# The last down product of a three-block transformer kernel as seven block products, with weight sums made in DRAM

## The chip, the cores and the metric

The kernel runs on one core of one Trainium2 chip. The metric is the device time of one execution in microseconds (us). The kernel before takes 3527.75 us, the median of three runs (3526.47 to 3527.91).

## The reference

Three pre-norm blocks follow one another on a sequence of 1024 tokens with 1024 features, all in float32. Cut to what matters here:

```python
def first_block(x, ...):       # 16 meta tokens ahead of x
    p = rms_norm(h) @ w_in     # q, k, v, g, gate rank, conv channels
    mix = concat(gla_branch(q, k, v, g, gr), short_conv_branch(cb, cc, cx))
    h = h + mix @ w_out;  h = h + relu(rms_norm(h) @ w_up) ** 2 @ w_down
def second_block(x, ...):      # three mixers, then a gated FFN with a convolution
def third_block(x, c, ...):
    x = x + gate1 * rms_norm_3(mix, norm1_post)
    h = rms_norm_3(x, norm2_pre) * (1.0 + scale2) + shift2
    f = jnp.square(jax.nn.relu(h @ w_fc1)) @ w_fc2
    return x + gate2 * rms_norm_3(f, norm2_post)
```

The FFNs are called f1, f2 and f3 in the kernel. The change concerns `f @ w_fc2` of the third block: a hidden vector of 4096 features times a 4096 x 1024 matrix, for 1024 tokens.

## The kernel before, in words

Features lie on partitions, so a tensor of 1024 x 1024 is eight tiles [128, 1024], or in halves of 512 tokens. A float32 product is made of three matmuls of rounded halves: with w = whi + wlo and x = Hh + Hl, `mm3` (L428) issues Hh·whi, Hl·whi and Hh·wlo into one accumulation in PSUM. Each weight unit of 512 KB is loaded by SP into a tile `raw` (L183) and split by `split` (L336): ACT copies it to `whi`, and DVE subtracts to get `wlo`. The class `Stream` holds the list of all units of the program in order. `tick` splits the next one when its load is some microseconds of PE time old, and `_split` (L203) then loads on, two units ahead.

**The FFNs.** `up7` (L895) makes an up product in groups. Of four blocks (two of output features by two of tokens) it needs seven block products instead of eight, with sums of weight blocks made by DVE on the raw tiles. For f1 and f3 every finished block goes through ReLU and square on ACT and from there to a DRAM tile `gd` (its issue is L910, from ACT). There are 16 groups; the first 12 of f3 take one piece from an earlier pass through the DRAM tile `sd` (L963). `down7` (L1029) makes the down product in chunks of 2, 2 and then 4 hidden tiles: the H tiles come back from `gd` as units of their own and are split into Hh and Hl, every chunk multiplies them with its weights for all eight output tiles, and `add` adds the sums to X, the first time by an ACT copy, later by DVE (L305). That is 32 hidden tiles x 8 output tiles x 2 halves x 3 = 1536 matmuls of 128x512. In f1 and f2 the residual is added by accumulating DMAs from POOL (L1066). In f3 it is loaded by SP into spare slots and a tile `hp` (both named `xr`), and `tail` normalises each half and writes the output, the second half in two parts of 256 tokens.

**The first block** is where the scheduler puts new rows. SP loads x (`xin`, eight loads of 256 or 512 KB) and the first weights; ACT squares x (`xs`), DVE makes the row factors (`rs`, `rr`, `xt`), ACT rounds the normed x (`Hh`). Then come the projections for v, q and k, g (`mm` into `V`, `kk`, `q`, `sg`) and the conv channels (`c1`: `cct`, `yt`). `gla` (L1348) is a generator that runs beside the projections, in four groups of 256 tokens, gi = 0 to 3. Each group has seven levels: `elem` (L1378) makes a factor `f` (POOL subtracts, ACT takes the exponential, DVE multiplies twice), `pairs` (L1428) makes eight small matmuls into each of two PSUM tiles `pa` and copies them into `At` by two DVE `copy_predicated` (L1437). States `hs` are carried by DVE; at a group's end `po` collects the output on PE and `norm` scales it into `sg`. After the first block's projections o1 multiplies `yt` and `sg` by w_out (into `X0`, `X1`).

**What sets the order.** The program is written in one order of calls, with generators advanced beside the matmuls by an estimate of PE time (`pe`). The framework's scheduler then orders the instructions of each engine by priorities and its own estimate of times, and gives every buffer and DMA a semaphore. Engines run their instructions in that order, and an instruction that waits holds those behind it.

## Time and profile before

| what | value |
|---|---|
| median of three runs | 3527.75 us |
| the profiled execution | 3526.44 us, of which span 3524.6 us |
| PE busy | 3419.4 us, 97% of the span, 16725 matmuls |
| DVE, ACT, POOL busy | 62%, 39%, 10% |
| mean granted clock of TensorE | 0.983 of full speed |
| DMA | 421.46 MB, mean 120 GB/s |

The busy time of PE is of modelled ends, but with 97% the matmuls follow one another nearly everywhere: a matmul less is worth its step, and a wait costs only where PE stands. The stages that the text speaks of lie at 0 to 60 us (start), 60 to 400 us (projections and GLA of the first block), 2843 to 3135 us (f3 up), 3135 to 3510 us (f3 down) and 3510 us to the end (tail).

### The profile page before, as it was taken

What the parts mean: (1) busy time and instruction counts of PE and PEld (TensorE: products, weight loads), DVE (VectorE), ACT (ScalarE), POOL (GpSimd) and SP (SyncE); (2) the same over time, 40 slices, a digit from 0 to 9 for tenths busy, and PEclk for the clock granted to TensorE, in tenths of its full rate; (3) what the DMA queues carried; (4) which work ended last, traced back from release to release, by engine and by line L of the source; (5) the groups of instructions that cost most, each with busy time, mean ns of one, the idle gap of its engine ahead of it and who ended that gap; (6) DMA issues with size and microseconds to landing.
All of it is one profiled execution on the core that took longest, in us unless ns stands there. A gap on an engine that the chain in (4) does not pass through costs nothing. (4 is left out here: it accounts for less than half of the span.)

```text
span 3524.6 us, 43683 instructions
## 1 busy us (share of the span) xinstructions
PE 3419.4 (97%) x16725; PEld 2808.1 (80%) x16725; DVE 2201.8 (62%) x3747; ACT 1367.4 (39%) x2046; POOL 335.8 (10%) x368
## 2 busy tenths in 40 slices
PE   7999999999999989999999999999999999999998
PEld 7788898887888777876698788878778878877887
DVE  5456366556666574667768988867665676645444
ACT  3432244444112443555634444431332564451111
POOL 0111020000000210000020000000232410000003
PEclk9999999999999999998999999999999999999999
DMA  3111444336633186444325322274222154343222
GB/s 106 48 43 47 148 135 148 117 118 191 184 133 113 58 196 173 123 129 147 110 94 166 116 84 84 96 221 149 88 67 90 62 184 149 132 167 114 96 84 72
DMA packets 180964, 421.46 MB, mean 120 GB/s; under 512 B 18088, under 2 KB 58744, under 8 KB 180628
## 3 DMA queue, kind: packets, MB, share of 16 engines
q1 hardware_dynamic: 133044, 325.34, 28.8%
q10 hardware_dynamic: 38304, 67.13, 5.1%
q0 software_dynamic: 9408, 26.22, 3.6%
q8 instruction: 131, 2.15, 0.3%
q14 instruction: 77, 0.63, 0.1%
HBM read 304.50 MB, written 105.63 MB: 116 GB/s over the span
## 5 line engine op out<-in xcount | busy, mean ns | idle before, releaser
L324 PE MATMUL mm<-Hh,whi 128*128 128x512 f32 (+3 forms) x3632 | 1384.2, 381 | 11.7 <-DVE X L305 4.5
L324 PE MATMUL mm<-Hh,wlo 128*128 128x512 f32 (+3 forms) x3632 | 1365.6, 377 | 4.7 <-DVE wlo L305 4.7
L324 PE MATMUL mm<-Hl,whi 128*128 128x512 f32 (+3 forms) x3632 | 1369.6, 377 | 0.2 <-DVE Hl L305 0.2
L324 PEld LDWEIGHTS mm<-Hh,whi 128*128 128x128 f32 x3632 | 686.0, 189 | 155.3 <-issue 6.8
L324 PEld LDWEIGHTS mm<-Hh,wlo 128*128 128x128 f32 x3632 | 685.7, 189 | 138.5 <-DVE wlo L305 9.0
L324 PEld LDWEIGHTS mm<-Hl,whi 128*128 128x128 f32 x3632 | 686.1, 189 | 127.7 <-issue 1.4
L319 ACT ACTIVATE whi<-raw 128x1024 fp32r<-128x1024 f32 (+3 forms) x386 | 379.0, 992 | 694.6 <-PE mm L324 459.9
L305 DVE TENSOR_TENSOR wlo<-raw,whi 128x1024 fp32r<-128x1024 f32 (+3 forms) x386 | 441.7, 1151 | 193.3 <-ACT whi L319 182.8
L305 DVE TENSOR_TENSOR X<-X,mm 128x512 f32<-128x512 f32 (+1 forms) x446 | 290.3, 655 | 366.7 <-PE mm L324 362.1
L324 PE MATMUL mm<-t,whi 128*128 128x512 f32 x1296 | 408.6, 396 | 2.4 <-ACT whi L319 2.4
L324 PEld LDWEIGHTS mm<-t,whi 128*128 128x128 f32 x1296 | 242.9, 188 | 62.4 <-ACT whi L319 3.3
L324 PE MATMUL mm<-t,wlo 128*128 128x512 f32 x648 | 256.7, 396 | 1.9 <-DVE wlo L305 1.7
L319 ACT ACTIVATE Hh<-raw 128x1024 fp32r<-128x1024 f32 x86 | 89.6, 1057 | 364.8 <-PE mm L324 213.3
L321 ACT ACTIVATE X<-X 128x512 f32<-128x512 f32 (+1 forms) x226 | 151.9, 673 | 186.2 <-DVE X L310 153.7
L305 POOL TENSOR_TENSOR acc<-acc,sq 128x256 f32<-128x256 f32 (+1 forms) x108 | 115.9, 1074 | 910.0 <-ACT sq L321 906.4
L305 DVE TENSOR_TENSOR raw<-raw 128x512 f32<-128x512 f32 x216 | 145.2, 687 | 79.5 <-DMA raw<-in_w_up 77.1
L324 PEld LDWEIGHTS mm<-t,wlo 128*128 128x128 f32 x648 | 121.8, 188 | 33.4 <-DVE wlo L305 4.1
L305 DVE TENSOR_TENSOR Hl<-raw,Hh 128x1024 fp32r<-128x1024 f32 x86 | 104.6, 1222 | 56.9 <-ACT Hh L319 56.3
L310 DVE SCALAR_TENSOR_TENSOR ada<-raw,silc,ada 128x128 f32<-128x128 f32 x336 | 115.5, 350 | 8.3
L324 PE MATMUL mm<-whi,Hh 128*128 128x264 f32 (+4 forms) x336 | 111.7, 342 | 6.5 <-ACT Hh L319 2.8
L324 PE MATMUL mm<-wlo,Hh 128*128 128x264 f32 (+4 forms) x336 | 111.2, 340 | 2.4 <-DVE wlo L305 2.4
L310 DVE SCALAR_TENSOR_TENSOR X<-mm,X 128x512 f32<-128x512 f32 x108 | 74.5, 690 | 61.6 <-PE mm L324 60.1
(290 smaller groups left out, 3400.0 us busy)
## 6 DMA issues: line engine op xcount, KB each, us to landing
raw<-in_w_up SPq DMA_DIRECT2D x136, 512.0 KB
raw<-gdf SPq DMA_DIRECT2D x86, 512.0 KB
raw<-in_w_down SPq DMA_DIRECT2D x86, 512.0 KB
gdf<-X ACTq DMA_DIRECT2D x108, 256.0 KB
raw<-in_w_ada SPq DMA_DIRECT2D x48, 512.0 KB
gdf<-X ACTq DMA_DIRECT2D x22, 512.0 KB
B<-qd SPq DMA_DIRECT2D x36, 256.0 KB
A<-qd SPq DMA_DIRECT2D x36, 256.0 KB
```

The source lines that it names most:

```text
L305: eng.tensor_tensor(out=out, in0=a, in1=b, op=op)
L310: self.nc.vector.scalar_tensor_tensor(out=out, in0=a, scalar=s, in1=b, op0=op0, op1=op1)
L319: self.nc.scalar.activation(out, in_, f, scale=scale, **kw)
L321: self.nc.scalar.activation(out, in_, f, bias=bias, scale=scale, **kw)
L324: self.nc.tensor.matmul(out, l, r, start=s, stop=e, skip_group_check=grp)
```

## The change

The down product of f3 is cut into blocks: two of hidden features by two of output features by two of tokens would be eight block products, and seven products P1 to P7 of sums of blocks give the same. Each has 8 pairs of units (`e`) x 4 output tiles x 2 x 3 = 192 matmuls, 1344 together.

- **Weights.** `_quarters` lays w_fc2 out by quarters. P1, P2 and P4 take a quarter as it is. P5, P6, P7 and P3 need sums of quarters, `sw[0]` to `sw[3]`, which `sums` (line 666 of the changed kernel) makes in DRAM: 16 copies of 1 MB issued from ACT, then 16 accumulating DMAs of 1 MB issued from POOL, of which eight add another quarter and eight add one finished sum to the next. In the source they stand ahead of the up product of f2, one at a time, 12 or 20 us of PE time apart.
- **Activations.** In the f3 up product each of the 16 groups makes four more DVE operations on 128x512 (two `tt`, two `stt`), 64 in all, and writes seven pieces of 256 KB to DRAM instead of four: three from ACT, four from POOL. Of the first 12 groups one piece is read back by POOL.
- **The down product.** `down_parts` walks P1, P2, P6, P7, P4, P5, P3. Each pair is a weight unit and a hidden unit of 512 KB, both split: 112 units, where `down7` had 64. PSUM sums run on over two products, and `out` makes X by an ACT copy or one DVE operation, so the adding up of chunks (L305, X<-X,mm) goes. Stream loads four units ahead.
- **The residual** is loaded by two POOL DMAs of 2 MB at the start of the down product, and the tail of the second half is one part of 512 tokens.

The core of the diff:

```diff
+    def sums(self, name, w):
+        S = self.S[name + "s"]
+        act, pool = self.nc.scalar, self.nc.gpsimd
+        for i, q in ((0, 1), (2, 1), (1, 0), (3, 2)):
+            for e in range(4):
+                self.sums_todo.append((act, 12.0, S[i, 2 * e:2 * e + 2], w[e, q], {}))
+        for i, q in ((0, 3), (2, 0), (1, None), (3, None)):
+            for e in range(4):
+                r = slice(2 * e, 2 * e + 2)
+                src = w[e, q] if q is not None else S[0 if i == 1 else 1, r]
+                self.sums_todo.append((pool, 20.0, S[i, r], src,
+                                       dict(accum_op=ALU.add, max_dma_last_dim=4096)))
+    def sums_step(self):
+        if self.sums_todo and self.pe >= self.sums_at:
+            eng, pace, dst, src, kw = self.sums_todo.pop(0)
+            eng.dma_start(out=dst, in_=src, **kw)
+            self.sums_at = self.pe + pace
...
-                relu2(v, v, 2 * g, 1)
+                if parts:
+                    relu2(v, v)
+                    t1_, t2_, t4_ = slot(), slot(), slot()
+                    self.tt(t1_, ca, v, ALU.subtract)
+                    self.tt(v, c22, v, ALU.subtract)
+                    self.stt(t2_, t1_, -1.0, c22, ALU.mult, ALU.subtract)
+                    self.stt(t4_, t2_, -1.0, c21, ALU.mult, ALU.subtract)
+                    for i, t in ((3, t1_), (5, v), (4, t2_), (6, t4_)):
+                        nc.gpsimd.dma_start(out=piece(i, g), in_=t)
...
+    def down_parts(self, name, out, tail):
+        W.ahead = 4
+        for n, i in enumerate(self.ORDER):
+            if n == 6:
+                self.drop_raws()
+                W.ahead = 2
+            if new:
+                ps = [self.ps() for _ in range(4)]
+            for e in range(8):
+                wa, wb = (W.get(u) for u in D_[8 * n + e])
+                for m in range(4):
+                    for k in (0, 1):
+                        w, x = slice(k * 512 + m * P, k * 512 + m * P + P), slice(k * 512, k * 512 + 512)
+                        self.mm3(ps[m], wa.hi[:, w], wa.lo[:, w], wb.hi[:, x], wb.lo[:, x],
+                                 new and e == 0 and k == 0, e == 7 and k == 1, not new)
...
+        self.sums("f3", a["w3_down"])
         self.up7("f2")
...
-        self.hp, e = self.pool("hp2", 1, None, "right")
+        xr = self.Hh.bitcast(F32)
+        for k in (0, 4):
+            nc.gpsimd.dma_start(out=xr[:, k:k + 4, :T], in_=self.xd[:, k:k + 4])
...
-        self.down7("f3", add, tail, quarters=True)
+        self.down_parts("f3", out, tail)
```

**Where the built program has the sums.** They depend on nothing but inputs, and the scheduler has put them at the start. On ACT, at the very start, before (whi is a rounded weight of v, Hh the rounded x, silc belongs to the third block):

```order
L321 ACT_TABLE_LOAD
L321 ACTIVATE xs_145<-xin_129 128x4x128
L321 ACTIVATE xs_146<-xin_129 128x4x128
L321 ACT_TABLE_LOAD
L321 ACTIVATE silc_62<-smalls_58 128x8
L319 ACTIVATE whi_151<-raw_137 128x1056
L321 ACT_TABLE_LOAD
L321 ACTIVATE rs_162<-rv_160 128x1
L321 ACTIVATE xs_171<-xin_129 128x4x128
L319 ACTIVATE whi_207<-raw_139 128x1056
L321 ACTIVATE xs_172<-xin_129 128x4x128
L319 ACTIVATE Hh_86<-xt_193 128x4x128
```

and now, from `rs` on (two xs, whi, two xs and whi stand ahead of it, and the first copy ahead of those):

```order
L334 ACT_TABLE_LOAD
L334 ACTIVATE rs_163<-rv_161 128x1
L334 ACT_TABLE_LOAD
L334 ACTIVATE silc_62<-smalls_58 128x8
L683 DMA swf3_103<-in_w3_down 16x16384
L334 ACT_TABLE_LOAD
L334 ACTIVATE rs_183<-rv_181 128x1
L332 ACTIVATE Hh_86<-xt_194 128x4x128
L332 ACTIVATE Hh_86<-xt_201 128x4x128
L332 ACTIVATE whi_230<-raw_156 128x1056
L332 ACTIVATE whi_236<-raw_212 128x1056
L683 DMA swf3_103<-in_w3_down 16x16384
```

The first Hh now stands behind two more table loads and the second of the 16 copies, whose DMA shares its semaphore with one of the x loads and waits for that. The other copies follow among the rows of the projections; the sixteenth stands right behind the exponential of f_1435 in group gi = 0.

On POOL, 14 of the 16 accumulates stand ahead of the GLA's first row; the last two stand among the rows of gi = 0. Before, from the fifth level of gi = 0 on (f_1659 is the first level of gi = 1):

```order
L305 TENSOR_TENSOR f_1505<-b_118 128x64x4 x2
L305 TENSOR_TENSOR ke_1794<-b_118 128x512
L305 TENSOR_TENSOR f_1565<-b_118 128x128x2 x2
L305 TENSOR_TENSOR f_1615<-b_118 128x256 x2
L305 TENSOR_TENSOR f_1659<-b_118 128x8x32 x2
```

and now:

```order
L683 DMA swf3_103<-swf3_103 256x1024
L318 TENSOR_TENSOR f_1506<-b_119 128x64x4 x2
L318 TENSOR_TENSOR f_1566<-b_119 128x128x2 x2
L318 TENSOR_TENSOR f_1616<-b_119 128x256 x2
L683 DMA swf3_103<-swf3_103 256x1024
L318 TENSOR_TENSOR f_1660<-b_119 128x8x32 x2
```

The last accumulate, which needs the last copy and an earlier accumulate to have landed, stands ahead of the first row of gi = 1.

On ACT the exponentials of gi = 1 have moved with it. Before they stood among the projections for sg and c1 (`cct`):

```order
L321 ACTIVATE f_1659<-f_1659 128x512
L321 ACT_TABLE_LOAD
L321 ACTIVATE sg_888<-mm_1590 128x512
L321 ACT_TABLE_LOAD
L321 ACTIVATE f_1714<-f_1714 128x512
L319 ACTIVATE whi_1678<-raw_1457 128x1024
L321 ACT_TABLE_LOAD
L321 ACTIVATE sg_888<-mm_1634 128x512
L321 ACT_TABLE_LOAD
L321 ACTIVATE f_1896<-f_1896 128x512
L319 ACTIVATE cct_1687<-mm_1689 128x348
```

and now (yt_3129 is the last tile of c1, whi_3463 a weight of o1):

```order
L332 ACTIVATE yt_3129<-cct_3128,smalls_58 128x1024
L332 ACTIVATE Hh_86<-yt_3129 128x512
L332 ACTIVATE whi_3463<-raw_3276 128x1024
L332 ACTIVATE Hh_86<-yt_3129 128x512
L334 ACT_TABLE_LOAD
L334 ACTIVATE f_1660<-f_1660 128x512
L334 ACTIVATE f_1715<-f_1715 128x512
L334 ACTIVATE ke_1795<-ke_1795 128x512
L334 ACTIVATE f_1897<-f_1897 128x512
L332 ACTIVATE kT_1883<-ax_1880 128x256
```

Groups gi = 1 to 3 stand behind the whole of c1, on every engine. DVE has their 42 `copy_predicated`, 36 products for `f`, 48 for `hs` and the rest in one run, and PE has from the last `mm` of c1 to the last `po` of gi = 3 their matmuls and 37 matmuls of o1, 24 of them ahead of the first `pa`.

## Rows read from the trace of the kernel before

**Rows 1.** The page: busy time of PE and of DVE over the span.

```profile
PE 3419.4 (97%) x16725; PEld 2808.1 (80%) x16725; DVE 2201.8 (62%) x3747; ACT 1367.4 (39%) x2046; POOL 335.8 (10%) x368
```

**Rows 2.** Busy times by stretch, f3 up to the end: stretch and length, then PE, PEld, DVE, ACT, POOL busy us (x instructions), granted clock, DMA share of 16 engines, GB/s.

```profile
3000.00:3135.00 135.00, 135.00 (x582) 108.94 (x581) 75.03 (x98) 61.53 (x88) 0.95 (x2) 1.00 0.37 125
3135.00:3181.00 46.00, 42.73 (x180) 32.74 (x178) 24.78 (x26) 29.65 (x40) 0.00 (x0) 1.00 0.70 234
3181.00:3300.00 119.00, 118.99 (x513) 96.27 (x514) 57.99 (x71) 20.46 (x20) 0.00 (x0) 1.00 0.31 102
3510.00:3524.60 14.60, 1.28 (x7) 0.93 (x6) 10.05 (x28) 0.20 (x1) 6.00 (x8) 0.64 0.44 144
```

**Rows 3.** The chain of waits at the start of f3 down (start us, us, what).

```profile
3143.14 12.03 DMA raw<-in_w_down
...
3158.97 4.38 DMA raw<-gdf
```

**Rows 4.** DMA from 3135 to 3181 us: GB/s in 40 slices of 1.15 us, and the issue of the residual.

```profile
GB/s 0 0 0 61 363 118 278 253 191 219 349 399 410 403 408 424 419 420 403 128 71 356 210 267 21 96 335 121 324 36 53 299 175 289 178 278 335 289 335 68
...
xr<-xd SPq DMA_DIRECT2D x1, 2048.0 KB
```

**Rows 5.** The groups of DVE in 2884 to 3060 us, f3 up, by form (x count, busy us, mean ns, idle before and its releaser).

```profile
L305 DVE TENSOR_TENSOR X<-mm,X 128x512 f32<-128x512 f32 x24 | 16.5, 688 | 7.1 <-PE mm L324 7.0
L310 DVE SCALAR_TENSOR_TENSOR X<-mm,X 128x512 f32<-128x512 f32 x22 | 15.2, 692 | 15.6 <-PE mm L324 15.2
```

**Rows 6.** Busy times by stretch in f2 up (columns as in rows 2).

```profile
2000.00:2050.00 50.00, 50.00 (x217) 40.36 (x216) 46.24 (x54) 23.10 (x26) 0.00 (x0) 1.00 0.24 88
1950.00:2000.00 50.00, 45.98 (x193) 35.53 (x192) 47.15 (x57) 20.94 (x21) 2.16 (x4) 1.00 0.41 139
```

**Rows 7.** The groups of DVE in the tail, 3509 us to the end, by form.

```profile
L310 DVE SCALAR_TENSOR_TENSOR X<-X,gp,ax 128x256 f32<-128x256 f32 x16 | 7.1, 472 | 0.5 <-PE ax L324 0.4
L305 DVE TENSOR_TENSOR X<-X,xr 128x256 f32<-128x256 f32 x8 | 3.5, 433 | 0.0
```

**Rows 8.** Busy times by stretch, start and first block (columns as in rows 2).

```profile
0.00:10.00 10.00, 1.01 (x4) 0.93 (x4) 1.65 (x6) 5.27 (x7) 0.22 (x4) 1.00 0.81 247
10.00:20.00 10.00, 5.20 (x20) 4.60 (x21) 7.87 (x24) 6.73 (x10) 0.00 (x0) 1.00 0.95 309
20.00:30.00 10.00, 9.23 (x64) 8.66 (x63) 7.95 (x17) 3.58 (x5) 0.00 (x0) 1.00 0.72 195
30.00:40.00 10.00, 7.45 (x60) 7.01 (x59) 7.99 (x20) 4.39 (x6) 0.00 (x0) 1.00 0.07 27
110.00:150.00 40.00, 40.00 (x177) 31.80 (x176) 16.57 (x23) 19.11 (x27) 7.81 (x9) 1.00 0.12 40
200.00:250.00 50.00, 49.17 (x376) 43.01 (x375) 33.12 (x65) 15.24 (x22) 9.03 (x14) 1.00 0.11 38
```

**Rows 9.** ACT at the start, in order of time (start us, us, what; in brackets idle before it and what ended it).

```profile
11.14 0.20 ACT L321 ACTIVATE rs<-rv 128x1 f32<-128x1 f32 x1
...
15.30 0.63 ACT L319 ACTIVATE Hh<-xt 128x512 fp32r<-128x512 f32 x1 [1.94 <-DVE xt L310]
...
25.54 1.07 ACT L319 ACTIVATE whi<-raw 128x1056 fp32r<-128x1056 f32 x1
```

**Rows 10.** DMA from 2300 to 2400 us, f2 down: the queues (packets, MB, share of 16 engines) and the accumulating DMAs of the residual (median us from issue to landing).

```profile
q0 software_dynamic: 2112, 4.19, 24.2%
...
X<-xd POOLq DMA_DIRECT2D x4, 1024.0 KB, 13.7
```

**Rows 11.** The groups of DVE in 150 to 365 us by form, the GLA beside the projections.

```profile
L1437 DVE COPY_PREDICATED At<-lvl,pa 128x512 f32<-128x512 uint8 x56 | 38.0, 731 | 34.9 <-PE pa L324 34.8
L310 DVE SCALAR_TENSOR_TENSOR hs<-hs,dec,ax 64x128 f32<-64x128 f32 x64 | 22.2, 346 | 3.7 <-PE ax L324 1.9
L305 DVE TENSOR_TENSOR f<-f,kk 128x256 f32<-128x256 f32 x21 | 8.9, 423 | 8.3 <-ACT f L321 8.3
```

**Rows 12.** PE's matmuls of the GLA from the end of gi = 0 to the first levels of gi = 1, in order of time (start us, us, what; each row ends where the next one begins, or a matmul of the projections between them).

```profile
199.09 1.95 PE L324 MATMUL po<-At,V 128*128 128x128 f32 x16
200.96 2.00 PE L324 MATMUL po<-qe,hs 64*128 64x64 f32 x32
202.90 0.43 PE L324 MATMUL mm<-Hh,whi 128*128 128x348 f32 x1
...
204.92 0.95 PE L324 MATMUL ax<-ones,sq 128*128 128x1 f32 x8
...
213.68 0.38 PE L1462 MATMUL ax<-ident,ke 128*128 128x128 f32 x2
213.99 1.16 PE L324 MATMUL pa<-f 64*128 64x128 f32 x16
215.08 1.16 PE L324 MATMUL ax<-ident,rr 128*128 128x128 f32 x8
...
218.08 1.14 PE L324 MATMUL ax<-V,kT 64*128 64x256 f32 x8
```

**Rows 13.** Busy times by stretch ahead of f3 up (columns as in rows 2).

```profile
2830.00:2840.00 10.00, 8.12 (x38) 6.32 (x36) 9.82 (x22) 8.19 (x21) 4.60 (x6) 1.00 0.34 120
2840.00:2850.00 10.00, 7.73 (x20) 5.21 (x21) 3.46 (x6) 4.48 (x8) 3.95 (x4) 0.66 0.58 196
```

More of the change, by code (lines that the diff above doesn't have):

```diff
@@ L161, in __init__ @@
         self.raws = []
+        self.ahead = 2
         self.groom = [False, False]
@@ L241, in _split @@
         self.ns += 1
-        while self.nd < min(self.ns + 2, len(self.seq)):
+        while self.nd < min(self.ns + self.ahead, len(self.seq)):
             self.load()
@@ L965, in start @@
                     nc.gpsimd.dma_start(out=ca[:, :512], in_=cd[g])
+                elif parts:
+                    nc.gpsimd.dma_start(out=ca, in_=piece(0, g))
             return s1, ca
@@ L1027, in up7 @@
         self.open_ss()
+    def down_parts(self, name, out, tail):
+        W = self.W
+        D_ = self.S[name + "d"]
+        sp, e = self.pool("sums", 1, None, "right")
+        self.ffn_es.insert(0, e)
+        s = sp.tile([P, 4, 512], F32, name="s_")
+        v = sp.tile([P, 4, 512], F32, name="v_")
+        W.ahead = 4
+        new = True
+        for n, i in enumerate(self.ORDER):
[4 more added lines that the diff above has]
+                ps = [self.ps() for _ in range(4)]
+            for e in range(8):
+                wa, wb = (W.get(u) for u in D_[8 * n + e])
[4 more added lines that the diff above has]
+                                 new and e == 0 and k == 0, e == 7 and k == 1, not new)
+                    if m == 3:
+                        W.done(wa)
+                        W.done(wb)
+                    if e == 7:
+                        z = ps[m]
+                        if i == "P1":
+                            self.act(s[:, m], z, AF.Copy)
+                        elif i == "P2":
+                            out(0, m, z, 1)
+                        elif i == "P6":
+                            self.tt(v[:, m], z, s[:, m], ALU.add)
+                        elif i == "P7":
+                            self.tt(s[:, m], z, s[:, m], ALU.add)
+                        elif i == "P4":
+                            out(0, 4 + m, z, -1, s[:, m])
+                        elif i == "P5":
+                            out(1, 4 + m, z, -1, s[:, m])
+                        else:
+                            out(1, m, z, 1, v[:, m])
+                    W.tick()
+                    if m % 2:
+                        self.step()
+                    else:
+                        self.fine()
+            new = i not in ("P1", "P6", "P5")
+            if i == "P4":
+                self.unsummed = True
+                self.norms[0] = self.bg(tail((0, 0, 512)))
+            elif i == "P3":
+                self.unsummed = True
+                self.norms[1] = self.bg(tail((1, 512, 1024)))
     def down7(self, name, add, tail, quarters=False):
@@ L1032, in down7 @@
         D_, Gu = self.S[name + "d"], self.S[name + "h"]
-        residual = 0 if name == "f3" else 4
+        residual = 4
         c = 0
@@ L2231, in block3, with out @@
         self.open_ring("f3d")
[L2232 to L2233 removed]
+        xr = self.Hh.bitcast(F32)
+        for k in (0, 4):
+            nc.gpsimd.dma_start(out=xr[:, k:k + 4, :T], in_=self.xd[:, k:k + 4])
         ac = []
[L2236 to L2265 removed]
+        got = [0, 0]
+        def out(half, m, z, sign, extra=None):
+            x = self.X[half][:, m]
+            if extra is None:
+                self.act(x, z, AF.Copy)
+            elif sign > 0:
+                self.tt(x, z, extra, ALU.add)
+            else:
+                self.stt(x, z, -1.0, extra, ALU.mult, ALU.subtract)
+            if not got[half]:
+                ac.append(self.acc())
+            self.sq_add(ac[half], x, got[half])
+            got[half] += 1
         def tail(part):
@@ L2270, in tail @@
             self.unsummed = False
-            if half and len(xr) < 2:
-                t = self.hp.tile([P, KT, 512], F32, tag="h0", name="xr")
-                self.dma(t, self.xd[:, :, 512:])
-                xr.append([t[:, k] for k in range(KT)])
             yield self.after(1.0)
```

81 lines of the change are left out of this document (41 added, 40 removed).

## The prediction

> **What bounds the kernel now.** The page's first part gives the engines' shares: PE is busy 97% of the span [rows 1], so the span is PE's matmuls plus some 105 us in which PE stands, and any edit is priced as matmuls less, or as new standing time. The busy times by stretch then show where PE stands and what could make it stand more: f3 up and most of f3 down are full, at 119.0 us for 513 matmuls, 0.232 us each [rows 2]; the first 40 us are not, with PE at 22.9 us and the DMA engines at 0.81, 0.95 and 0.72 in the first three slices [rows 8]. In the first block the GLA hides beside the projections: at 200 to 250 us PE is busy 49.2 of 50 and DVE 33.1 [rows 8]. Groups of DVE and PE's order in time give the prices of the GLA [rows 11, 12], and the chain of waits shows what holds f3 down at its beginning [rows 3].
>
> **The change, part by part.** The profiled execution took 3526.4 us, 1.3 less than the median of the three runs; I sum against the former.
>
> *Matmuls of f3 down.* 1344 in place of 1536: 192 x 0.232 = **-44.5 us**. PE was full there, so this is all on the path.
>
> *The beginning of f3 down.* Before, 46 us held 42.7 us of PE work [rows 2]: 3.3 us lost, in waits for loads of 12.0 and 4.4 us, the longer one behind the 2 MB residual load [rows 3, 4]. Now 4 MB of residual stand in POOL's queue at the same place, about 10 us at the 400 to 420 GB/s that the single one reached [rows 4], beside loads twice as dense. It could lose nothing at all (POOL's transfer shares with loads that are issued earlier, four ahead): -3; or each of the two transfers holds a load as the one did, 12 us against the 4 units of lead: +8. I take **+3**.
>
> *Twice the loads in f3 down.* A pair of units is 1.05 MB per 24 matmuls (5.57 us): 188 GB/s, where 102 was drawn [rows 2]. The same queue gave 289 to 335 GB/s in many slices of 512 KB loads [rows 4], so I cost it at 0; the other end is a rival. The splits are 112 in place of 64 weights and 32 + 32 hidden halves, about as many; the adds of chunks go. DVE stood at 58 of 119 us there and has room [rows 2].
>
> *f3 up.* 16 groups x 4 DVE operations of 0.69 us [rows 5] = 44 us more over 292 us. DVE was busy 75 of 135 us [rows 2], 56%, and a little more in the shorter first twelve groups: 2.75 us more per group of 13.9 us (60 matmuls) takes those to some 80 to 87%. f2 up ran so: DVE at 46.2 of 50 us with PE full, and in the stretch ahead 47.2 with PE at 46.0 [rows 6]. The first row gives 0, the second 4 us per 50, over 167 us 13. I take **+2** (0 to 10), near the first, since DVE here stays under both. The three more piece writes a group and the re-read piece go mostly to POOL's queue, on which only a load per group stood.
>
> *Tail.* One part of 512 tokens in place of the last 256: eight `stt` and eight `tt` of 0.69 us [rows 5] in place of 0.47 and 0.43 [rows 7], half of the `tt` on POOL: **+1.5** (0 to 4).
>
> So f3 alone gives -44.5 + 3 + 2 + 1.5 = **-38**.
>
> *The sums at the start.* The order puts them there and not in f2. The trace has no copy from DRAM to DRAM; the nearest row is the start's own rate, 309 GB/s [rows 8]: 3.4 us per MB of all 16 engines. For an accumulate it is the residual's: four of 1 MB took 24.2% of 100 us, so 6.05 us each, and 13.7 to landing [rows 10]. Two or three of each fall in the first 30 us, 19 to 28 us of engine time, where 25 of 30 us are taken already [rows 8]. What PE waits for there are x loads, weights and the chain over ACT and DVE: the first Hh at 15.3 us and the fourth whi at 25.5 [rows 9]. ACT's new order sets two table loads and a copy that waits for an x load ahead of the first Hh: it comes about 4.5 us later by the durations, and the loads for the fourth whi up to 10. Between 2 (only the table load stays) and 20 (most of the transfers push the chain back) I take **+10**.
>
> *The sums beside the projections.* 16 x (3.4 + 6.05) = 151 us of DMA engine time in the first 180 us or so; the rows show the engines nearly empty from 30 us on (0.07, later 0.12) [rows 8]. They fit, but each load now waits behind megabytes: **+4** (0 to 20). POOL's f rows wait for the accumulates ahead of them to be issued, not to land, which is in this.
>
> *The GLA.* This is the largest term, and nothing in the diff speaks of it. Groups gi = 1 to 3 run after the last matmul of c1. Their DVE work is 42 copies x 0.73 + 48 hs x 0.35 + 36 f x 0.42 = 62.6 us [rows 11], and with ke, qe, sg, the row factors and the four Hl of sg some 15 more: 77. Waits within: before, DVE waited 34.9 us for pa at 28 levels [rows 11], 1.25 each with PE busy on projections; at 21 levels that is 26 at most, 0 at least; I take 15, as PE is now free but only two pa tiles are in use. With the last po (3.8 us) the run takes 96 us. PE has in it: per group seven pa (1.09 each), po 3.8, and ones, ident, rr and V,kT twice each (0.9, 0.31, 1.1, 1.1) [rows 12], 18.2 us, three times that less one pa that stands earlier, 53.4, and 13 matmuls of o1, 3.0. The other 24 matmuls of o1 cover the run's beginning (last yt, Hh, table load, f: about 5 us). PE stands 96 - 56.4 = **+40** (24 without waits, 50 with all). DVE's time that comes free in c1 is worth nothing: PE is full there.
>
> *Clock.* In 2840 to 2850 us the granted clock was 0.66, a mean of the levels at 1.2 and 2.4 GHz, after ten microseconds with PE at 8.1 [rows 13], while 30 to 40 us with PE at 7.45 kept 1.00 [rows 8]. The GLA's run has PE at about 60%: **+3** (0 to 12).
>
> Sum: -38 + 10 + 4 + 40 + 3 = +19; 3526.4 + 19 = 3545.4, and with the median's 1.3 above, about **3546 us**.
>
> The Trainium skill, page "DMA: Bandwidth & Descriptors", section "Issuing engines are not separate DMA queues", says that transfers issued by ScalarE, SyncE or GpSimd share the same 16 engines and interleave, so that issuing the copies from ScalarE buys no bandwidth. The trace agrees so far as POOL's accumulates took their 24.2% from the 16 engines that SP's loads use [rows 10]. Were ACT's copies apart from SP's loads, the start's term would be the table load's 2, and the sum 3538. The same page's section "Anatomy of one DMA" fits a GpSimd transfer by 2.0 us plus its bytes at 436 GB/s: an estimate of 4.4 us per MB, where the trace has 13.7 to landing for an accumulate. By it the accumulates would load the engines 26 us less, and the term of the projections would be nearer 2.
>
> **Rivals.** *The sums are free and DVE runs through (faster).* The start hides the copies, because its chain is ACT's and DVE's (DVE at about 8 of 10 us from 10 us on [rows 8]), and the GLA's run closes at DVE's own busy time: -38 + 2 + 24 = -12, 3515 us. It decides where start, projections and GLA together stay under 31 us (38 less 7). For it: the DVE waits in rows 11 come in part from matmuls that PE now doesn't have. Against it: the levels form a chain (f, pa, copy) of which DVE holds only a part, and PE has no other work. Chance 0.22.
>
> *f3 down is bound by its loads (slower still).* 56 pairs are 58.7 MB. Were the supply beside the splits no more than 160 GB/s, they would take 367 us in place of 312, and f3's gain is gone: about 3546 + 55 = 3601. Break-even with the old 356 us of matmuls is at 165 GB/s. For it: 0.70 of the DMA engines at 234 GB/s while PE waited [rows 2]; against: 289 to 335 in the slices without a wait [rows 4]. Chance 0.10.
>
> *The clock falls in the whole GLA run.* PE's 56 us of work would take up to twice that and bind the run: 112 + 4 of 96, some 20 us more, 3563. For and against: rows 13 and rows 8 as above. Chance 0.10. The Trainium skill, page "TensorE: Matmul & The Clock Gate", Part 1, says that the low level is the default and that activity releases it; by that rule gaps as dense as here would bring the fall, and the row at 30 to 40 us speaks against it.
>
> *It does what its source says, not what the order shows.* With the sums spread over f2 as written, the first block would be as before: -38 + 3, about 3492. The built order speaks against it: 0.04.
>
> **How the numbers follow.** The forecast's own case has 0.54, with a range of 3528 to 3568. About 7 us (0.2%) is what a measurement can tell from no change: faster is below 3520.7, slower above 3534.8. Faster: 0.17 of the first rival and 0.04 of the last, 0.21. Same: the rest of the first, 0.05, and 0.08 of the forecast's lower end, 0.13. Slower: 0.46 + 0.10 + 0.10, 0.66. The range takes in the first rival and the clock and leaves out most of the load-bound case: 3508 to 3585.
>
> **What would show it.** Right: copies and accumulates from 0 to about 170 us; the first `Hh` near 20 us; PE at 0.5 to 0.65 in a stretch of some 96 us after the last `yt`, ended by `pa` waiting for `f` and `At`; f3 down at 1344 matmuls, 312 to 320 us, DMA near 188 GB/s. Wrong: a GLA run under 80 us or with PE over 0.8; PE waiting for `raw` throughout f3 down; DVE over 95% in f3 up.

## The result, and the profile after

The kernel before took 3527.1 us (3526.3 to 3527.9, 4 runs on that chip), the changed one **3565.8** (3563.1 to 3573.5, 4 runs): a ratio of 1.0113 [1.0096, 1.0131], slower by 38.6 us where +19 was forecast. The profiled execution is the slowest of the four (3573.5, span 3571.7), so the sums below come to 47.1, the difference of the two spans, and not to 38.6.

The page's engine line, which answers to [rows 1]:

```profile
PE 3411.0 (95%) x16437; PEld 2800.4 (78%) x16437; DVE 2224.8 (62%) x3725; ACT 1399.8 (39%) x2072; POOL 393.9 (11%) x452
```

PE has 288 instructions fewer: 192 products of 128x512, and 96 because the last part of f3 down no longer goes in halves of 256 tokens. It stands 161 us where it stood 105. Yet its busy time fell by 8 us only, not by the 44.5 of the matmuls that went. Where, the busy times by stretch tell (columns as in rows 2; a DMA share over 1 comes of transfers that reach past their stretch), which answer to [rows 2, 8]:

```profile
0.00:10.00 10.00, 0.58 (x3) 0.58 (x3) 1.42 (x4) 2.54 (x3) 1.32 (x5) 1.00 0.80 273
10.00:20.00 10.00, 0.43 (x3) 0.35 (x2) 1.33 (x2) 1.80 (x3) 0.00 (x0) 1.00 1.06 269
20.00:30.00 10.00, 3.40 (x12) 2.71 (x12) 6.98 (x24) 7.24 (x10) 0.00 (x0) 1.00 1.00 332
30.00:40.00 10.00, 8.51 (x52) 7.83 (x51) 6.04 (x14) 5.42 (x7) 0.89 (x1) 1.00 1.04 305
60.00:80.00 20.00, 15.56 (x105) 14.85 (x104) 9.37 (x22) 4.99 (x7) 1.75 (x2) 0.83 1.05 251
110.00:150.00 40.00, 33.97 (x191) 28.23 (x191) 10.81 (x20) 15.23 (x25) 3.75 (x6) 0.87 0.84 226
...
350.00:400.00 50.00, 44.32 (x289) 39.45 (x289) 28.95 (x55) 13.58 (x20) 6.56 (x10) 0.95 0.29 95
400.00:450.00 50.00, 42.06 (x326) 38.17 (x324) 35.21 (x76) 16.59 (x27) 12.70 (x21) 0.70 0.00 1
450.00:500.00 50.00, 46.64 (x313) 39.56 (x312) 29.11 (x62) 13.17 (x20) 9.70 (x10) 0.97 0.38 132
3000.00:3050.00 50.00, 45.09 (x191) 35.38 (x190) 32.85 (x48) 19.10 (x27) 9.77 (x18) 1.00 0.57 202
3050.00:3100.00 50.00, 44.55 (x184) 33.75 (x183) 33.63 (x50) 18.64 (x27) 9.76 (x18) 1.00 0.53 186
...
3240.00:3280.00 40.00, 40.00 (x173) 32.26 (x172) 18.89 (x17) 16.63 (x18) 0.54 (x1) 1.00 0.84 312
3300.00:3350.00 50.00, 50.00 (x216) 40.25 (x216) 21.46 (x18) 22.44 (x26) 4.34 (x3) 1.00 0.57 188
```

Three places stand out. At the start the DMA engines are full for 110 us, where they had been nearly empty from 30 us on. From 350 to 500 us the late GLA holds PE at 42 to 47 of 50. In f3 up PE is at 45 of 50, with DVE at 33 only. f3 down is full, its beginning too, at the DMA share forecast.

Two milestones cut the first block. The rows of tile V (duration min/median/max in ns, first and last start in us) of the changed kernel:

```profile
L332 ACT ACTIVATE V<-mm x9: 379/390/391, 38.5 to 124.3; 128x264 f32<-128x264 f32 x8, 16x264 f32<-16x264 f32 x1
L337 PE MATMUL po<-At,V x64: 272/311/581, 239.2 to 469.8; 128*128 128x128 f32 x64
```

and of the kernel before:

```profile
L319 ACT ACTIVATE V<-mm x9: 371/391/393, 29.3 to 83.3; 128x264 f32<-128x264 f32 x8, 16x264 f32<-16x264 f32 x1
L324 PE MATMUL po<-At,V x64: 272/275/275, 199.1 to 364.4; 128*128 128x128 f32 x64
```

V begins 9 us later and ends 41 later, in 85.8 us where it took 54. f1 up writes its first half at 564.7 us, before at 496.0: the first block lost **68.6 us**. Its busy times up to that write, before and now:

```profile
0.00:496.00 496.00, 475.26 (x3189) 419.62 (x3190) 259.81 (x523) 179.40 (x270) 68.73 (x95) 1.00 0.24 80
0.00:564.70 564.70, 499.97 (x3189) 446.35 (x3190) 256.90 (x523) 172.05 (x265) 80.08 (x111) 0.94 0.45 130
```

The same 3189 matmuls keep PE busy 25 us longer, at a granted clock of 0.94 in place of 1.00, and PE stands 44 us more.

f3 up, from its first matmul on hidden halves to its last, went from 248.4 to 267.3 (**+18.9**), f3 down from 368.0 to 318.7 (**-49.3**), the tail from 16.1 to 21.1 (**+5.0**); the remaining 3.9 of the 47.1 lie in the rest of the program.

### The profile page after: what moved, and what is told of

Its sections match the earlier page's. It is cut to its first block, busy times and chain, and to the rows that moved or that the text cites. A ratio compares the mean times of both kernels' runs of the same rounds, so it can differ in the third digit from the quotient of the medians.

```text
span 3571.7 us, 43368 instructions
## 1 busy us (share of the span) xinstructions
PE 3411.0 (95%) x16437; PEld 2800.4 (78%) x16437; DVE 2224.8 (62%) x3725; ACT 1399.8 (39%) x2072; POOL 393.9 (11%) x452
## 5 line engine op out<-in xcount | busy, mean ns | idle before, releaser
L337 PE MATMUL mm<-Hh,whi 128*128 128x512 f32 (+3 forms) x3088 | 1173.6, 381 | 18.0 <-DVE X L318 13.5
L337 PE MATMUL mm<-Hl,whi 128*128 128x512 f32 (+3 forms) x3088 | 1163.1, 377 | 0.2 <-DVE Hl L318 0.2
L337 PE MATMUL mm<-Hh,wlo 128*128 128x512 f32 (+3 forms) x3088 | 1159.8, 376 | 3.1 <-DVE wlo L318 3.1
L318 DVE TENSOR_TENSOR wlo<-raw,whi 128x1024 fp32r<-128x1024 f32 (+3 forms) x466 | 544.9, 1181 | 357.3 <-ACT whi L332 346.8
L337 PEld LDWEIGHTS mm<-Hh,whi 128*128 128x128 f32 x3088 | 584.1, 189 | 135.4 <-DVE X L318 18.4
L337 PEld LDWEIGHTS mm<-Hh,wlo 128*128 128x128 f32 x3088 | 583.6, 189 | 115.1 <-DVE wlo L318 6.4
L318 POOL TENSOR_TENSOR acc<-acc,sq 128x512 f32<-128x512 f32 (+1 forms) x102 | 117.3, 1152 | 668.3 <-ACT sq L334 634.9
L337 PE MATMUL mm<-whi,wlo 128*128 128x512 f32 x448 | 176.9, 395 | 0.0
L337 PE MATMUL mm<-wlo,whi 128*128 128x512 f32 x448 | 176.9, 395 | 0.0
L337 PE MATMUL mm<-whi 128*128 128x512 f32 x448 | 176.7, 394 | 0.0
```

The lines of the kernel that those rows point to most:

```text
L318: eng.tensor_tensor(out=out, in0=a, in1=b, op=op)
L337: self.nc.tensor.matmul(out, l, r, start=s, stop=e, skip_group_check=grp)
```

## The experiments

A run of the kernel before stood beside each (3526.8 to 3529.7 us); times are medians in us, differences are against *no_sums* (3497.2) where nothing else is said.

### What f3's edits are worth alone

**no_sums.** P5, P6, P7 and P3 read plain quarters; the copies and accumulates go, and with them the new order of the first block.

```diff
-A.update({"P5": sw[0], "P6": sw[1], "P7": sw[2], "P3": sw[3]})
+A.update({i: [a[down][e // 2, q, e % 2] for e in range(8)]
+          for i, q in (("P5", 1), ("P6", 3), ("P7", 1), ("P3", 2))})
-        self.sums("f3", a["w3_down"])
```

> The 16 copies and 16 accumulating DMAs are left out; P5, P6, P7 and P3 multiply plain quarters (same loads, same matmuls, the sums of weights are not in the result). ACT, PE and DVE of the first block then have the order of the kernel before. Theory 1 (everything lost before f3 comes from the sums; in the changed kernel's profile 68.6 us by the end of the first block): 3527 - 49 (f3 down) + 19 (f3 up) + 5 (tail) = 3502, range 3497 to 3510, first sdf write at 496 us as before. Theory 2 (a good part is lost for other reasons): over 3530.

Measured: 3497.2, 0.9912 [0.9897, 0.9927]. f3's own edits give 31 us; all that the change loses beyond that, 68.5 us, hangs on how the sums are made. (f1 up begins at 497.7 here.)

**late_sums** and **late_noops.** One small DMA that reads X ties the sums to the start of f2 up, so the first block keeps its order; late_noops also drops the four DVE operations of each f3 group and writes the pieces from tiles that are there.

```diff
 def sums(self, name, w):
+    act.dma_start(out=S[:, 0::2, 0, 0, 0:1], in_=self.X[1][0:4, 7, 0:4].unsqueeze(2))
# late_noops, in f3 up
-self.tt(t1_, ca, v, ALU.subtract)   # and v, t2_, t4_
```

> All sums as in the changed kernel, but one small DMA first writes an element of each of their regions from X as it stands after the second block's o2, so no copy can be placed ahead of f2; the order of the first block is that of the kernel before. Theory 1 (their place was what cost, f2 has room for them): within 8 us of the kernel without sums, 3502 to 3512. Theory 2 (their 150 us of DMA engine time cost about as much wherever they are, beside f2's loads now): 3530 to 3560.

> The kernel with late sums, with the four DVE operations of each f3 up group left out (the pieces are written from other tiles, so that every DMA stays; the sums of activations are not in the result). Theory 1 (f3 up became bound by DVE between a weight load and the next): f3 up as before, 15 to 19 us under the kernel with late sums. Theory 2 (the three more writes and the re-read hold the weight loads): within 5 us of the kernel with late sums, DVE waiting for in_w_up as long as now.

Measured: 3582.3, 1.0157 [1.014, 1.0175], beyond both theories, and 3568.1, 1.0113 [1.0093, 1.0132]. The sums cost 85 us in f2 up, more than at the start. The four operations cost 14 us: f3 up takes 264.9 us with them and 249.6 without. In late_noops (columns as in rows 2) PE is full at almost the same DVE time per stretch, 31 to 33 of 50:

```profile
3000.00:3050.00 50.00, 49.94 (x214) 39.86 (x213) 33.05 (x45) 23.80 (x34) 11.69 (x22) 1.00 0.68 222
3050.00:3100.00 50.00, 49.93 (x215) 39.90 (x214) 30.70 (x42) 22.74 (x32) 8.11 (x15) 1.00 0.59 195
```

So DVE is not busy too long; it stands in a chain. The chain of waits in f3 up of the changed kernel (start us, us, what):

```profile
3029.20 0.69 DVE wlo L318
3029.91 4.78 DMA raw<-in_w_up
3034.71 0.70 DVE raw L318
3035.48 0.57 issue
3036.05 0.68 DVE raw L318
3036.73 0.60 DVE X L318
3037.51 0.95 issue
3038.46 0.68 DVE X L318
3039.14 0.60 DVE X L323
3039.74 0.61 DVE X L318
3040.40 3.08 PE mm L337 x12
```

A split frees a raw tile, the load into it takes 4.8 us, its sum on DVE comes next, then DVE's work on the products in its order, then PE. An operation put into that chain lengthens the group here, though DVE is idle a third of the time.

**nosums_pool4.** no_sums with the four operations on POOL (four `tt`, one sign on ACT).

```diff
-self.tt(t1_, ca, v, ALU.subtract)
+self.tt(t1_, ca, v, ALU.subtract, gp)   # and t2_, t4_, v; then t2_ negated on ACT
```

> The kernel without sums, with the activation sums of f3 up made by POOL (four tensor_tensor of 1.3 us a group) and one ACT negation, none by DVE. Theory 1 (DVE's four operations bind f3 up): 12 to 16 us under the kernel without sums, 3481 to 3486, f3 up 250 us from its first to its last matmul on t. Theory 2 (POOL and DVE share their way to memory, so DVE slows by as much): within 5 us of it.

Measured: 3516.9, 0.9971 [0.9956, 0.9985], 20 us **worse** than on DVE, beyond both theories. DVE's own sums of weights in f3 up, by form, in no_sums:

```profile
L318 DVE TENSOR_TENSOR raw<-raw 128x512 f32<-128x512 f32 x48 | 31.5, 687 | 22.9 <-DMA raw<-in_w_up 22.6
L318 DVE TENSOR_TENSOR X<-mm,X 128x512 f32<-128x512 f32 x24 | 16.5, 687 | 18.7 <-PE mm L337 18.7
```

and in nosums_pool4:

```profile
L318 DVE TENSOR_TENSOR raw<-raw 128x512 f32<-128x512 f32 x47 | 52.1, 1116 | 35.6 <-DMA raw<-in_w_up 35.2
L318 DVE TENSOR_TENSOR X<-mm,X 128x512 f32<-128x512 f32 x23 | 15.7, 682 | 6.8 <-issue 5.6 <-PE mm L337 1.2
```

The DVE operation with both sources in SBUF grows from 687 to 1116 ns while POOL works, the one that reads a product from PSUM stays at 682.

### Is it the traffic, and which of its properties

**late_copies.** late_sums without the 16 accumulates. **late_copies_rows**, **after_rows.** The copies cut from 16 x 64 KB into 256 rows of 4 KB, in late_copies and in the changed kernel; the order of instructions on PE, DVE and ACT stays the same in both (by the traces, but for 4 places on PE in after_rows). **late_copies_pool.** late_copies with the copies issued from POOL.

```diff
# late_copies
-self.sums_todo.append((pool, 20.0, S[i, r], src, dict(accum_op=ALU.add, ...)))
+pass
# late_copies_rows, after_rows
-self.sums_todo.append((act, 12.0, S[i, 2 * e:2 * e + 2], w[e, q], {}))
+self.sums_todo.append((act, 12.0, S[i, 2 * e:2 * e + 2], w[e, q], dict(max_dma_last_dim=4096)))
# late_copies_pool
-self.sums_todo.append((act, 12.0, ...
+self.sums_todo.append((pool, 12.0, ...
```

> The kernel with late sums, with the 16 accumulating DMAs left out (the sums are then plain quarters). Theory 1 (the cost in f2 up goes by DMA engine time, 3.4 of 9.45 us per MB pair): 36% of the 75 to 85 us, so about 3497 + 28 = 3525. Theory 2 (a copy of 16 pieces of 64 KB holds an engine until its piece is done, and the load behind it waits longer than beside the accumulates' 4 KB rows): more than half remains, over 3540. Theory 3 (only the accumulates cost): under 3510.

> The change with its 16 copies cut into rows of 4 KB (256x1024 in place of 16x16384), bytes, times of issue and the order of the instructions on PE, DVE and ACT all as in the change. Theory 1 (a piece of 64 KB occupies a DMA engine for so long that the 512 KB weight loads beside it, which go in rows of 4 KB, wait behind pieces): the part of the first block's loss that is traffic goes, and only the order's part stays: 69 us fall to some 35, in all 3530 (3520 to 3542). Theory 2 (it is the bytes, whatever their form, and the order): as the change, 3566 (3560 to 3573).

> The kernel of the copies alone in f2 up (late_copies: no accumulates, so three of the four regions of sums hold plain quarters) with each copy cut into rows of 4 KB, order of all instructions as there. late_copies took 3552.8, 56 us over the kernel without sums (3497). Theory 1 (pieces of 64 KB): most of the 56 goes, 3500 to 3522. Theory 2 (bytes, and the order that the scheduler gives f2 up with ACT's issues in it): 3553 (3545 to 3560).

> The kernel of the copies alone in f2 up, pieces of 64 KB as there, but issued from POOL in place of ACT, so that they share a queue with POOL's loads of 256 KB and not with ACT's writes of 256 and 512 KB (three of the four regions of sums hold plain quarters). Theory 3 (ACT's own writes stand behind the copies in one queue, and tiles come free late): 3500 to 3520. Theory 1 (pieces of 64 KB hold SP's loads, whichever queue they come from): 3545 to 3560.

Measured: late_copies 3552.8, 1.0068 [1.0053, 1.0083], +56 for 16 MB of copies. That had spoken for large pieces, but after_rows is 3566.7, 1.0106 [1.0082, 1.013], and late_copies_rows 3555.7, 1.0076 [1.0056, 1.0096]: the size of the pieces changes nothing. From POOL it is 3579.0, 1.0139 [1.0115, 1.0164], dearer still, so to leave ACT's queue doesn't help; but the order of f2 moved too, by the traces at 623 of PE's 16437 positions. f2 up in late_copies:

```profile
1850.00:1950.00 100.00, 88.20 (x363) 69.21 (x362) 68.36 (x85) 38.96 (x50) 11.58 (x12) 0.95 0.59 202
1950.00:2050.00 100.00, 81.89 (x322) 62.65 (x320) 75.20 (x88) 31.07 (x31) 3.22 (x6) 0.95 0.43 147
```

and in no_sums:

```profile
1850.00:1950.00 100.00, 99.71 (x441) 80.67 (x440) 80.64 (x100) 45.85 (x58) 9.27 (x13) 1.00 0.50 161
1950.00:2050.00 100.00, 95.68 (x400) 75.23 (x399) 93.57 (x109) 42.89 (x44) 3.22 (x6) 0.98 0.34 116
```

PE loses 12 to 14 of 100 us at a mean DMA share of .43 to .59. The mean rate is not what runs out. Two waits of each kernel (us in total, times, longest), in late_copies (DVE in 1850 to 2100 us, PE in 1850 to 2150):

```profile
DVE raw L318 <- DMA raw<-in_w_up: 13.9, 10, 2.3
PE mm L337 <- DVE wlo L318: 27.8, 11, 4.7
```

and in no_sums (1790 to 2040 us):

```profile
DVE raw L318 <- DMA raw<-in_w_up: 5.4, 3, 3.7
PE mm L337 <- DVE wlo L318: 2.2, 4, 0.7
```

DVE's waits for loads grew by 8.5 us, PE's for the splits by 25.6. By the traces the matmuls of the two kernels also stand at other places in 479 of 16437 positions, all of them between 1850 and 2145 us; what of the 56 us is that, these runs do not tell.

### Is there a stage that takes the sums for little

Each of these holds all 32 DMAs until another stage, by a small DMA that reads what that stage has ready. **f1_sums**: f1 up. **f1_spread**: the same with a pace of 48 us in the source. **att_sums**: attention of block 2. **f1d_chain**: f1 down, all from POOL, copy and accumulate in turn. **start_sp**: the start, but the copies from SP.

```diff
# f1_sums
+self.sums("f3", a["w3_down"])     # with late_sums' small DMA
 self.up7("f1")
# att_sums, f1d_chain: the small DMA reads augA, or f1's last hidden unit
# start_sp
-self.sums_todo.append((act, 12.0, ...
+self.sums_todo.append((self.nc.sync, 12.0, ...
```

> As the kernel with late sums, but gated and called ahead of f1's up product, so that copies and accumulates run beside f1 up and f1 down, where DVE is busy 50 to 65% and not 82 to 92% as in f2 up. Theory 1 (f2 up lost its time because its chain from load over DVE has no room, the same traffic is cheaper where DVE has some): 10 to 40 us over the kernel without sums, 3507 to 3537. Theory 2 (traffic costs its engine time wherever it is): 60 to 85 us over it, 3557 to 3582.

> The kernel with the sums held until f1 up (f1_sums, 3578.1, 81 us over no sums), with the pace four and two and a half times slower (48 us of PE time between any two of the 32 DMAs, so that they reach over some 1500 us, from f1 up into f2). Theory 1 (each copy that meets loads costs some 2 to 3 us, so the sum is the same however thin they lie, as long as loads run there; attention's part is free): 3545 to 3570. Theory 3 (it is the crowding: two or three DMAs of 1 MB under way at a time, with accumulates behind them): 3500 to 3520.

> All 32 copies and accumulates, but held (by one small DMA that reads augA) until the attention of block 2, where PE is full for 25 of 25 us in most slices and no product waits for a weight load in a pair of raw buffers; paced at 9 and 10 us of PE time. The order of the first block is that of the kernel before. Theory 1 (the sums cost where weight loads are on the path: a load that meets a copy lands late, and each raw tile has one spare only): 8 to 25 us over the kernel without sums (3497), 3505 to 3525. Theory 2 (32 MB of traffic beside any stage costs 55 to 80 us): 3555 to 3580.

> All 32 DMAs issued from POOL, copy and accumulate in turn, held until f1 up's last unit is written, so that they run beside f1 down and the start of block 2; since each accumulate makes POOL wait until its copy has landed, no more than two are under way at a time. Theory 3 (crowding: several DMAs of 1 MB under way at once make the weight loads late): 10 to 25 us over the kernel without sums (3497), 3507 to 3522. Theory 1 (each of them costs some 2 to 3 us beside any stage that loads weights): 3555 to 3580.

> The change with the 16 copies issued from SP in place of ACT: they stand in SP's queue behind the loads of x and the first weights, the order of the first products (V) and of the three later GLA groups on PE, DVE and ACT is that of the kernel before, and the accumulates lie on POOL between GLA's own operations. Theory A (at the start most of the loss is the order that the scheduler makes round ACT's issues, and the traffic costs little there, since the first block needs hardly a load after 40 us): 3505 to 3528. Theory B (the traffic itself): 3550 to 3575.

Measured: f1_sums 3578.1, 1.014 [1.0125, 1.0155]; f1_spread 3578.5, 1.0142 [1.0127, 1.0157]; att_sums 3627.7, 1.0284 [1.0267, 1.0301]; f1d_chain 3618.2, 1.0262 [1.0244, 1.028]; start_sp 3666.3, 1.0398 [1.0383, 1.0414]. All are slower than the change, and four of the five (all but f1_sums) came out beyond what either theory gave. f1_spread told nothing on spreading: its copies (row of the sums' tile) are issued in 277 us, in f1_sums in 261, whatever the pace, since the scheduler moves up what nothing holds:

```profile
L684 ACTq DMA_DIRECT2D swf<-in_w_down x16: 496/496/611, 491.3 to 768.2; - x16
```

att_sums' were moved up in the same way, to 1223 us, ahead of attention. f1d_chain meets a stage that draws .48 of the DMA engines by itself (900 to 1050 us in no_sums), and there they run full:

```profile
900.00:1050.00 150.00, 71.20 (x287) 57.44 (x286) 57.62 (x121) 16.28 (x16) 17.24 (x23) 0.72 0.92 260
```

In start_sp the copies stand among the weight loads in SP's queue until 687 us, and so does all that is late behind them. Of the stages tried none takes 32 MB for less than 69 us; each of these prices holds the order that came with the sums there.

**sbuf_sums.** No copies: f3 down loads the quarters themselves and adds them on DVE ahead of the split.

```diff
+B = {"P6": (Q[0], Q[1], Q[3]), "P7": (Q[0], Q[1]), "P5": (Q[1], Q[3]), "P3": (sw, Q[2])}
+elif u.kind == "s":
+    k.tt(src, src, g.r1, ALU.add)
+    if u.keep is not None:          # P6's sum, for P3
+        k.nc.gpsimd.dma_start(out=u.keep, in_=src)
```

> All sums made where they are used, in f3 down, without copies and accumulates: 40 more weight loads of 512 KB, each added on DVE into the raw tile before its split (P6 of three quarters, P7 and P5 of two, P3 of q2 and of P6's sum, which is kept in DRAM). By the rows of f3 down without sums (PE full, DMA share .58 at 189 GB/s, DVE 21 to 25 us of 50), 24 MB more and 40 additions of some 1.3 us. Theory A (there is room in f3 down, and a load there has four raw tiles of lead): 3500 to 3517. Theory B (P6 with 32 loads and P3 with 32 and two raw tiles are bound by their loads): 3520 to 3545.

Measured: 3560.1, 1.0082 [1.0065, 1.0099], +63, beyond both theories. P6 and P3 are bound by their loads, by more than I gave them: P6 takes 81 us and P3 61, in place of 45 each. In P6 SP waits 35 us for the writing of its sums out of the raw tile (SP's wait in us, times, longest; then the busy times of most of P6, and from there on into P3):

```profile
SPq L191 <- DMA swf<-raw: 35.0, 8, 6.4
3258.00:3334.00 76.00, 55.28 (x186) 41.85 (x185) 33.97 (x29) 15.67 (x18) 8.91 (x10) 0.82 0.71 232
3334.00:3490.00 156.00, 150.58 (x652) 121.16 (x652) 108.09 (x103) 60.25 (x63) 25.32 (x14) 0.99 0.78 257
```

### The first block: order or traffic

**bulk_start.** no_sums with 32 plain copies of 1 MB from POOL at once, at the start. **gla_late.** no_sums with gi = 1 to 3 of the GLA held until c1 is done, as in the change. **v_serial.** no_sums with the norm of each token group of V, from the fourth on, held until the group before is copied. **order_only.** The edits of v_serial and gla_late together: most of both orders, no traffic.

```diff
# bulk_start
+for i in range(4):
+    for e in range(8): nc.gpsimd.dma_start(out=..., in_=w3_down[...])     # 1 MB each
# gla_late
+while gi == 1 and not self.c1_done:
+    yield
# v_serial, in in_norm, from 512 tokens on
+self.stt(ps[:p, :nt], self.V1[:p, min(c0, T) // P - 1, 510:510 + nt], 0.0, ps[:p, :nt], ALU.mult, ALU.add)
```

> The kernel without sums, with 32 plain 1 MB copies between DRAM tiles issued by POOL one after another at the start: as many bytes to write as all the sums, unused. ACT, PE and DVE keep the order of the kernel before. Theory 1 (the changed order of the first block cost most of the 68.6 us, traffic only the 9 to 15 us up to the first weights): 3507 to 3520. Theory 2 (traffic ahead of the x and weight loads cost most of the 41 us lost by the last V): 3540 to 3560. POOL's first f row stands behind the issues only.

> The kernel without sums, in which the GLA's group gi = 1 waits, in the program's order of calls, until the last tile of c1: gi = 1 to 3 then stand behind c1 on every engine, as in the changed kernel, and no copy or accumulate runs. Theory 1 (the order alone makes the exposed GLA run): 20 to 35 us over the kernel without sums (3497), 28 by the changed kernel's trace. Theory 2 (the run was long because the sums' traffic and a low clock slowed it): under 10 us over it.

> The kernel without sums (3497; three of the four regions of sums hold plain quarters), with no added traffic, in which the norm of each token group of V from the fourth on waits for the V copy of the group before (one small DVE operation ties them), so that on PE, DVE and ACT the norm stands behind the whole group, as it does in the change. Theory A (the change's V phase is long by that order): V's first to last goes from 54.7 to 75 to 90 us (85.8 in the change), in all 3515 to 3532. Theory B (it is long by the traffic of the sums beside it): under 65 us, 3497 to 3508.

> Both orders of the change's first block and none of its traffic: the edits of v_serial (+17 over no sums, 3497) and of gla_late (+13) in one kernel (three of the four regions of sums hold plain quarters). Theory A (the order and the traffic are two terms that add): 3497 + 17 + 13 = 3527 (3520 to 3534), which leaves 39 of the change's 69 us in the first block to the traffic. Theory B (the late GLA run takes the V phase's loss in, or the two together cost as much as the change): under 3517, or over 3550.

Measured: bulk_start 3596.2, 1.0188 [1.0173, 1.0204], beyond both theories: V begins at 128.8 us, since SP's loads of x wait behind the flood, and from there it runs as before. gla_late 3510.2, 0.9944 [0.993, 0.9959]: +13, between its two theories. v_serial 3513.8, 0.9959 [0.9944, 0.9974]: +17, between its two theories. order_only 3529.1, 1.0001 [0.999, 1.0013]: +32 where 13 + 17 = 30 was expected. Tile V in order_only:

```profile
L332 ACT ACTIVATE V<-mm x9: 381/391/394, 29.9 to 102.3; 128x264 f32<-128x264 f32 x8, 16x264 f32<-16x264 f32 x1
L337 PE MATMUL po<-At,V x64: 272/275/421, 217.3 to 435.6; 128*128 128x128 f32 x64
```

Its stretches show what the serial V costs, with the DMA engines empty:

```profile
40.00:60.00 20.00, 14.89 (x107) 14.08 (x107) 8.99 (x25) 4.88 (x7) 0.00 (x0) 0.84 0.00 1
60.00:80.00 20.00, 15.63 (x115) 14.93 (x114) 8.47 (x24) 3.11 (x7) 0.00 (x0) 0.93 0.00 1
```

f1 up's first write falls at 530.4 us. Of the first block's 68.6 us, **34.4 are shown to be the order** (496.0 to 530.4), by the medians 31.8 of 68.5. The other **34.3** (530.4 to 564.7; by the medians 36.7) hold the traffic, but not it alone: order_only has not the whole order of the change. By the traces PE's matmuls stand at other places in 1406 of 16437 positions, all in the first block. The 34.3 lie in three parts, by the traces of the two kernels:

- **Ahead of V's beginning, 8.6 us.**
- **Within V, 13.4** (85.8 less 72.4). The third copy of V starts 14.1 us after the second, in order_only 10.0, because in the change the norm ahead of it stands behind the second copy too; that part of the order v_serial leaves out. From the third copy to the eighth it is 47.4 and 46.6 us, with the DMA engines full in the one and empty in the other. Some 3 us come at the second copy and 5.5 at the last, where DVE waits 4.5 us for a load (`lf`) ahead of Hl.
- **In the late GLA run, 12.0.** From V's last copy to the last matmul of c1 it is 241.9 and 241.6 us, from the run's last po to f1 up's first write 92.7 and 92.6. The run itself, from the first pa behind c1 to the last po, in the change and in order_only:

```profile
382.80:472.00 89.20, 72.22 (x611) 64.62 (x610) 67.89 (x150) 24.06 (x39) 22.90 (x36) 0.79 0.01 3
355.00:437.80 82.80, 72.11 (x643) 60.66 (x642) 65.78 (x147) 24.52 (x39) 23.41 (x36) 0.90 0.07 24
```

The DMA engines are empty there. The change has 13 matmuls of 128x512 in its run, order_only 37: the other 24, 5.6 us, stand ahead of it in the change, and its run is 6.4 us longer besides, at a lower clock. So these 12 us and the 4 at the third copy of V are read as order too, some 50 of 68.6 in all, which leaves the traffic at most some 18. That part is read from the traces and not tested: no run has the change's whole order without its traffic.

## Why the prediction was right and wrong

The direction held: f3 down gains its matmuls, and the first block, with its new order, loses more than that. The size was half of what came. The GLA's term, which was to carry the loss, was charged too much, and by that luck the sum hides a part of what other terms missed:

| term | forecast | by the profiles |
|---|---|---|
| f3 down, matmuls and beginning | -41.5 | -49.3 |
| f3 up | +2 | +18.9 |
| tail | +1.5 | +5.0 |
| the sums at the start | +10 | +41 (V's end) |
| projections, GLA, clock | +47 | +27.6 |
| rest of the program | 0 | +3.9 |

**The step that failed most is "The sums at the start".** It priced the way to the first Hh and the fourth whi. In the changed kernel they are (rows of ACT in order of time, as in rows 9):

```profile
27.07 0.63 ACT L332 ACTIVATE Hh<-xt 128x512 fp32r<-128x512 f32 x1 [1.01 <-DVE xt L323]
34.57 1.08 ACT L332 ACTIVATE whi<-raw 128x1056 fp32r<-128x1056 f32 x1 [0.37 <-DMA raw<-in_w_v]
```

Hh came 11.8 us later where 4.5 was said, whi 9.0 later where 10 was, and V began 9 later, close to the +10. The step ended there and took V's token groups for unchanged. But V's order had changed as that of the GLA had: the norm of the next group now stood behind the whole group on DVE and ACT, so each paid the chain from the root to Hl with PE waiting; the granted clock, after PE had stood so, was .83 in the mean from 40 to 100 us. That is 18 us without any traffic; of the 13 more in the change, some 4 are a norm more in that order. I had looked at the order for one late run and not asked what else the same cause had moved.

**f3 up** was priced by DVE's busy share: 80 to 87% expected, with f2 up's full stretch as the nearest row [rows 6]. The share was 67%, and PE still lost 5 of 50: the operations lie in the chain load, sum, product, of two raw tiles. [rows 5] had shown that DVE waits for PE there, 22.7 us in 176 ahead of two of its groups; a busy share does not tell whether new work falls into such waits or between a load and the matmuls that need it. late_noops sets the price at 14.

**The GLA.** The run behind c1 came, with the 13 matmuls of o1 that were counted and at nearly the length forecast, 89 us for 96. But PE stood in it 17 us and not 40, and was busy 72 of 89, 0.81: the sign of being wrong that the prediction had set, PE over 0.8. It had no more to do than the 56.4 us counted. The granted clock was 0.79, a mean of its levels of 1.2 and 2.4 GHz, and with PE partly at the lower one the same matmuls took some 16 us more (72 less 56), where +3 was charged. Standing and clock make 33 of the 43 forecast; held back alone, in gla_late, where the run has more matmuls to cover it, the GLA costs 13.

**The clock** fell in a part of that run, as its rival had it, but PE did not come to bind the run. In the whole first block it makes some 25 of the 68.6 us, by the busy times above; the forecast had +3 for it, in the GLA alone.

**f3 down** was right: 1344 matmuls in 318.7 us, DMA 188 GB/s as worked out, and the beginning that I charged with +3 gained 4.8 instead; that four raw tiles let the loads run ahead is the likely reason, which no run varies. "Bound by its loads" did not come, and "the sums are free" is what no_sums would be: they are not. **The projections'** +4 was not too low: from V's last copy to the end of c1 the change takes as long as order_only, with copies and accumulates beside it until 206 us. **The tail** was priced by DVE's operations alone: its last part took DVE 8.2 us in place of 5.9, and from there to the end it is 6.0 in place of 3.8.

What stays open: why 16 MB of copies cost 56 us in f2 up at half the DMA rate. The piece size is excluded, and issuing from POOL did not help; a load that comes late by one copy in a chain with one spare tile could do it, and so could the moved matmuls. The waits show 8.5 us more for loads, which is not the whole; no run separates the two. How much of the change's own 34.3 us beyond order_only is traffic is open in the same way, at most some 18 by the traces.

## What to carry to other kernels

When an edit adds instructions without inputs to wait for, look at every place whose order it moves, not only at the one that shows most; about half of the first block's loss here is shown to be order, with no byte moved, and by the traces it is more. Price work added to an engine by the chain that it lies in and the spare tiles of that chain, not by the engine's busy share. And bytes are not free because the DMA engines are idle on average: 32 MB cost 69 to 169 us in each of six places, the order that came with them included, and the gain that they served was 31.

## What was not expected of the hardware

POOL slows DVE: 1116 ns in place of 687 for a DVE sum of two SBUF tiles while POOL works, 682 with a PSUM source (above). The Trainium skill, page "GPSIMD Engine Reference", section "Specifications", says that the two share their SBUF interfaces, with contention where DVE has two SBUF inputs; the trace agrees. An accumulate of 1 MB within DRAM took 8.1 to 21.5 us to landing, 11.8 in the median, beside the 13.7 of the residual's [rows 10]. Pieces of 64 KB and of 4 KB cost the same (3565.8 and 3566.7).
